# Two-layer hybrid trunk: gate, branch and first-layer products written feature-major, and another order of columns at the head of the second layer

## The chip, the cores and the metric

The kernel runs on one core of one Trainium2 chip. The metric is device microseconds of one execution, the median of several runs. Everything is 32-bit floating point on the way in and out; matrix products are made in a rounded 32-bit type (fp32r in the profile), with each operand split into a high and a low part.

## The reference

Two layers work on 256 positions of width 1024. Each layer first mixes, then applies an MLP:

```
mod = silu(c) @ ada_w[l] + ada_b[l]            # sh1, sc1, g1, sh2, sc2, g2
h = rms_norm(x) * (1 + sc1) + sh1
proj = h @ w_in   # u, v | fox q k v f | moba q k v | ssm z, xbc, dt | gates
y_a = gelu(u) * (causal spatial product of layer_norm(gelu(v)))
y_b = forgetting attention(fox q, k, v, f)
y_c = causal attention with partial rotary (moba q, k, v)
y_d = Mamba-2 mixer(z, xbc, dt)
merged = sum_i sigmoid(gate_i) * (y_i @ w_branch_i)
x = x + g1 * (merged @ w_out)
x = x + g2 * (relu(rms_norm'(x) @ w1)^2 @ w2)
```

The output is the final RMSNorm of x.

## The kernel before, in words

**Weights.** All large weights come in units of 0.5 MB: two blocks of 128 rows by 512 columns. `stream()` lists them in the order of use, and between them the units of `ada_w`, which VectorE folds into an accumulator (`acc`, line 242). Each weight unit lands in one of five `raw` buffers, ScalarE casts it to its high part (`hi`, line 363) and VectorE subtracts to get its low part (`lo`, line 365). `ahead` fetches three units ahead of the one in use, six in four places where tiles of later stages are lent to it (`lent`: `hl`, `hq`). A chunk is four units: 1024 rows by 512 columns.

**Two forms of product.** With activations split as `xh`, `xl` and weights as `hi`, `lo`, each product is xh·hi + xh·lo + xl·hi. In the straight form (`gemm`, `unit_mms`, lines 419 to 421) the 128 by 128 activation block is the stationary operand and 512 weight columns stream past: 12 matmuls of 512 columns in a unit, and the result has positions on the partitions. In the turned form (`gemm_T`, lines 447 to 449) a 128 by 128 block of the weight is stationary and the 256 positions stream past: 24 matmuls of 256 columns in a unit, and the result has features on the partitions, all positions in the free axis. The chunks `z1` to `z3` of both layers, `z0` of the second, `fq`, `fk` and six of eight `w1` chunks are turned already. `by_tile` runs several straight chunks for the first 128 positions, then again for the second 128, so that the second half of the activations may come later.

**Order of a layer.** u, v (first layer: together with z0, in steps; second layer: `by_tile`), z0 to z3 (input of Mamba), `narrow`, then q, k, v of forgetting attention (`fq`, `fk`, `fv`), then four times `branch`: two gate chunks (`ga0`, `ga1`), and the branch's own products (`pa0`, `pa1`), in the order a (gMLP), d (Mamba), b, c (`mq`, `mk`, `mv` lie between d and b), then `o0`, `o1` (w_out) and the MLP. `add` (lines 1103 to 1106) multiplies a branch's product with its gate and adds it to the sum `mg`, which has positions on the partitions. In branch c, `merge_T` transposes `mg` on TensorE in eight groups of four (tile `mT`), and lines 1145 and 1146 split the result into `xhT` and `xlT`, the activations of `o0` and `o1`.

**Generators.** Mixers are Python generators: `start` enters one in the list `running`, and `pump`, called behind each unit of a product, steps all of them. `yield n` waits n units more. So Mamba's parts stand in the program as many units behind one another as units are pumped, and `drain(gen_d)`, called behind the gates of branch d, writes whatever of Mamba is left in one go. Mamba ends with a broadcast product `rb` (line 914), six multiplications from it (line 917) and the split into `yhd` and `yld` (lines 521 and 522), which branch d's products `pd0` and `pd1` read.

Each engine works in the order of its program. PSUM tiles of the products come from a pool of four banks (`gps`), those of the mixers from a pool of two (`xps`), transposes from another two.

Of the kernel before, what the change touches and what calls it, by code (L numbers as in the profile page):

```python
# [15 lines left out]
P = 128  # L16
# [27 lines left out]
def stream():  # L44
# [16 lines left out]
    for l in range(L):  # L61
# [23 lines left out]
        for nm, c0 in (("fq", C_FQ), ("fk", C_FK), ("fv", C_FV)):  # L85
            plan_chunk((l, nm), "w_in", l, c0, KT)
# [52 lines left out]
def trunk_kernel(ctx: ExitStack, tc: tile.TileContext, a: dict, out: bass.AP):  # L139
# [295 lines left out]
    def gemm_T(key, xs, alloc):  # L435

        ps = [alloc(f"pT_{key[0]}{key[1]}_{q}").rearrange("p (f c) -> p f c", f=2) for q in range(2)]
        for u in range(KT // 2):
            i = take(key, 1)[0]
            ahead(i)  # L440
            hi, lo = ready[i]
            for f in range(4):
                o = ps[f // 2][:, f % 2, :]
                for j in range(2):
                    k = 2 * u + j
                    c = slice(f * P, (f + 1) * P)
                    te.matmul(o, hi[j][:, c], xs[0][:, k, :], start=k == 0 and f % 2 == 0, stop=False)  # L447
                    te.matmul(o, hi[j][:, c], xs[1][:, k, :], start=False, stop=False)  # L448
                    te.matmul(o, lo[j][:, c], xs[0][:, k, :], start=False, stop=k == KT - 1 and f % 2 == 1)  # L449
            pump()  # L450
        return ps
# [65 lines left out]
    def yT_tiles(nm, n, tag):  # L517
        return by_pos([mp.tile([P, n, NT * P], F32R, tag=tag, bufs=2, name=f"y{w}{nm}") for w in "hl"])
# [123 lines left out]
    def qkv(l, nm, hT, rot):  # L642
# [11 lines left out]
        ps = gemm((l, nm + "v"), KT, hT)  # L654
        vt = []
        for t in range(NT):
            vt.append(tok(f"{nm}v{l}{t}"))
            s.copy(vt[t], ps[t])
# [3 lines left out]
    def gmlp(l, ps, ya):  # L662
        pr = params[l]
        us, vn = [], []
        for which, lst in ((0, us), (1, vn)):
            for t in range(NT):
                tk = tok(f"{'uv'[which]}{l}{t}")
                s.activation(tk, ps[which][t], AF.Gelu_apprx_tanh)
                lst.append(tk)
# [10 lines left out]
        for t in range(NT):  # L680
# [10 lines left out]
            uT = transposes(us[t], f"uT{l}{t}")  # L691
            v.tensor_tensor(tm, tm, uT, op=ALU.mult)
# [3 lines left out]

    def zx_post(l, n, ps, zs, xb):
        tks = []
        for t in range(NT):
            tk = tok(f"zx{l}{n}{t}")  # L700
            s.copy(tk, ps[t])
            tks.append(tk)
        yield 1
        for t in range(NT):
            tp = transposes(tks[t], f"zxT{l}{n}{t}")
            for lo_, hi_ in ((0, 2), (2, 4)):
                f0 = 4 * n + lo_
                if f0 < 6:
                    s.copy(zs[:, f0:f0 + 2, t * P:(t + 1) * P], tp[:, lo_:hi_, :])
                else:  # L710
                    s.copy(xb[:, f0 - 6:f0 - 4, 3 + t * P:3 + (t + 1) * P], tp[:, lo_:hi_, :])
            yield 0
# [301 lines left out]
    for l in range(L):  # L1014
        pr = params[l]
        res = {}
        if l == 0:
            full = fullp
            firsts = {nm: [gps(f"ps_0{nm}_{t}") for t in range(NT)] for nm in "uv"}

            def first_mms(f, nm, ts=range(NT)):
                if ts[0] == 0:
                    got[nm] = take((0, nm), 1)[0]
                for t in ts:
                    unit_mms(got[nm], t, firsts[nm][t], hT[t][0], hT[t][1], 2 * f - 2, f == 1, f == 4)

            got = {}
            for f in range(5):
# [22 lines left out]
                if f == 0:  # L1051
                    fetch_one()
                    firsts["z0"] = [xps(f"ps_0z0_{t}") for t in range(NT)]
# [18 lines left out]
        ya = yT_tiles(f"a{l}", 4, "y2")  # L1072
# [3 lines left out]
        yd = yT_tiles(f"d{l}", 6, "y3")  # L1076
        zx = []
        if pz is not None:
            zx = [start(zx_post(l, 0, pz, zs, xb), -1)]
# [8 lines left out]
        qT, kT, vt = qkv(l, "f", hT, False)  # L1088
        mg = [mp.tile([P, D], F32, tag="mg", bufs=2, name=f"mg{l}{t}") for t in range(NT)]

        def gates(br, n):
            pgt = gemm((l, f"g{br}{n}"), KT, hT)
            th = []
            for t in range(NT):
                h = tok(f"th{l}{br}{n}{t}")
                s.activation(h, pgt[t], AF.Tanh, scale=0.5)
# [3 lines left out]
        def add(br, n, t, th, pp):  # L1100
            dst = mg[t][:, n * 512:n * 512 + 512]
            if br == "a":
                v.scalar_tensor_tensor(dst, th[t], 1.0, pp[t], op0=ALU.add, op1=ALU.mult)
            else:
                v.scalar_tensor_tensor(th[t], th[t], 1.0, pp[t], op0=ALU.add, op1=ALU.mult)
                v.tensor_tensor(dst, dst, th[t], op=ALU.add)

        def branch(br, ys, before=None, last=None):
            ths = [gates(br, n) for n in range(2)]
            if before is not None:  # L1110
                before()
            if last is not None:
                def after(n):
                    def f(t, ps):
                        add(br, n, t, ths[n], {t: ps})
                        last(t, n)
                    return f
# [189 lines left out]
```

## Time and profile before

| | |
|---|---|
| runs | 1119.17, 1122.38, 1124.32 us; median 1122.38 |
| profiled execution | 1119.5 us, its span 1117.5 us |
| TensorE (PE) | 1089.8 us busy, 98% of the span, 6420 matmuls |
| weight loads of TensorE (PEld) | 913.2 us, 82% |
| VectorE (DVE) | 767.5 us, 69% |
| ScalarE (ACT) | 619.7 us, 55% |
| DMA | 234.62 MB, mean 210 GB/s |
| granted TensorE clock | 0.996 of full speed |

TensorE's busy time counts overlapping matmuls once; whether it advances at its full pace is read from the distance between the starts of its instructions, not from the share.

### The profile page before, as it was taken

What the parts mean: (1) busy time and instruction counts of PE and PEld (TensorE: products, weight loads), DVE (VectorE), ACT (ScalarE), POOL (GpSimd) and SP (SyncE); (2) the same over time, 40 slices, a digit from 0 to 9 for tenths busy, and PEclk for the clock granted to TensorE, in tenths of its full rate; (3) what the DMA queues carried; (4) which work ended last, traced back from release to release, by engine and by line L of the source; (5) the groups of instructions that cost most, each with busy time, mean ns of one, the idle gap of its engine ahead of it and who ended that gap; (6) DMA issues with size and microseconds to landing.
All of it is one profiled execution on the core that took longest, in us unless ns stands there. A gap on an engine that the chain in (4) does not pass through costs nothing.

```text
span 1117.5 us, 16674 instructions
## 1 busy us (share of the span) xinstructions
PE 1089.8 (98%) x6420; PEld 913.2 (82%) x6420; DVE 767.5 (69%) x1088; ACT 619.7 (55%) x975; POOL 37.2 (3%) x58
## 2 busy tenths in 40 slices
PE   6999999999999999999899999999999999999997
PEld 4799977777777789988788998777777777889985
DVE  3887657786778756566676685678768676555565
ACT  4566565565555555554464575656555456554463
POOL 0000002000000100000000000110000001000000
PEclk9999999999999999999999999999999999999999
DMA  9876553666666668677845655446666755666670
GB/s 373 310 234 188 186 173 133 199 226 200 226 218 224 197 206 287 230 262 256 294 155 185 211 175 169 167 148 213 221 209 208 236 187 180 190 206 227 206 245 38
DMA packets 65327, 234.62 MB, mean 210 GB/s; under 512 B 7256, under 2 KB 8024, under 8 KB 65248
## 3 DMA queue, kind: packets, MB, share of 16 engines
q1 hardware_dynamic: 64960, 233.30, 63.7%
q8 instruction: 50, 0.82, 0.3%
q10 hardware_dynamic: 288, 0.27, 0.1%
q14 instruction: 29, 0.24, 0.1%
HBM read 232.49 MB, written 1.05 MB: 209 GB/s over the span
## 4 chain that ended last, share of the span: by engine, by line
PE 81%; DMA 8%; DVE 7%; ACT 2%; issue 2%; POOL 1%; DVEq 0%; POOLq 0%; ACTq 0%; SPq 0%
DMA raw<-in_wpk_dram 7%; PE yps L419 4%; PE yps L420 4%; PE yps L421 4%; DVE lo L365 2%; PE pT_1w L447 2%; PE pT_1w L448 2%; PE pT_1w L449 2%; PE pT_1z L447 1%; PE pT_1z L448 1%; PE pT_1z L449 1%; PE pT_0w L449 1%; PE pT_0w L447 1%; PE pT_0w L448 1%; PE pT_0z L447 1%
## 5 line engine op out<-in xcount | busy, mean ns | idle before, releaser
L363 ACT CAST hi<-raw 128x1024 fp32r<-128x1024 f32 x319 | 333.7, 1050 | 323.7 <-PE yps L421 60.2
L365 DVE TENSOR_TENSOR lo<-raw,hi 128x1024 fp32r<-128x1024 f32 x315 | 382.2, 1222 | 159.4 <-ACT hi L363 158.4
L242 DVE SCALAR_TENSOR_TENSOR acc<-raw,csil,acc 128x1024 f32<-128x1024 f32 x70 | 89.9, 1284 | 93.2 <-DMA raw<-in_wpk_dram 93.1
L420 PE MATMUL yps<-lo,hh 128*128 128x512 f32 x232 | 91.7, 395 | 0.5 <-DVE lo L365 0.5
L419 PE MATMUL yps<-hi,hh 128*128 128x512 f32 x232 | 92.0, 397 | 0.0
L421 PE MATMUL yps<-hi,hl 128*128 128x512 f32 x232 | 91.6, 395 | 0.0
L449 PE MATMUL pT_0w<-xhT,lo 128*128 128x256 f32 x192 | 54.2, 282 | 0.1
L447 PE MATMUL pT_1w<-xhT,hi 128*128 128x256 f32 x192 | 54.0, 281 | 0.0
L447 PE MATMUL pT_0w<-xhT,hi 128*128 128x256 f32 x192 | 54.0, 281 | 0.0
L449 PE MATMUL pT_1w<-xhT,lo 128*128 128x256 f32 x192 | 53.9, 281 | 0.0
L448 PE MATMUL pT_1w<-xlT,hi 128*128 128x256 f32 x192 | 53.9, 281 | 0.0
L448 PE MATMUL pT_0w<-xlT,hi 128*128 128x256 f32 x192 | 53.9, 281 | 0.0
L419 PEld LDWEIGHTS yps<-hi,hh 128*128 128x128 f32 x232 | 43.5, 188 | 10.9 <-issue 1.0
L420 PEld LDWEIGHTS yps<-lo,hh 128*128 128x128 f32 x232 | 43.5, 187 | 10.7 <-DVE lo L365 0.9
L421 PEld LDWEIGHTS yps<-hi,hl 128*128 128x128 f32 x232 | 43.5, 187 | 10.6
L449 PEld LDWEIGHTS pT_0w<-xhT,lo 128*128 128x128 f32 x192 | 36.2, 188 | 0.5 <-DVE lo L365 0.5
L448 PEld LDWEIGHTS pT_1w<-xlT,hi 128*128 128x128 f32 x192 | 36.2, 188 | 0.3
L448 PEld LDWEIGHTS pT_0w<-xlT,hi 128*128 128x128 f32 x192 | 36.2, 188 | 0.3
L447 PEld LDWEIGHTS pT_0w<-xhT,hi 128*128 128x128 f32 x192 | 36.2, 188 | 0.3
L447 PEld LDWEIGHTS pT_1w<-xhT,hi 128*128 128x128 f32 x192 | 36.2, 188 | 0.3
L447 PE MATMUL pT_1z<-xhT,hi 128*128 128x256 f32 x128 | 36.3, 284 | 0.0
L449 PEld LDWEIGHTS pT_1w<-xhT,lo 128*128 128x128 f32 x192 | 36.2, 188 | 0.0
(608 smaller groups left out, 2760.5 us busy)
## 6 DMA issues: line engine op xcount, KB each, us to landing
raw<-in_wpk_dram SPq DMA_DIRECT2D x436, 512.0 KB, 4.3
x<-in_x_dram SPq DMA_DIRECT2D x2, 512.0 KB
wst<-in_big_dram SPq DMA_DIRECT2D x2, 512.0 KB
out_dram<-xnz SPq DMA_DIRECT2D x4, 256.0 KB
bsb<-in_big_dram SPq DMA_DIRECT2D x2, 256.0 KB
fw<-in_final_norm_w_dram SPq DMA_DIRECT2D x1, 512.0 KB
w<-in_big_dram SPq DMA_DIRECT2D x2, 128.0 KB
cst<-in_cst_dram ACTq DMA_DIRECT2D x1, 185.0 KB
```

What stands on the lines that cost most here:

```text
L242: v.scalar_tensor_tensor(acc[l, j], raw, csil[:, k:k + 1], acc[l, j], op0=ALU.mult, op1=ALU.add)
L363: s.copy(hi, raw)
L365: v.tensor_sub(lo, raw, hi.bitcast(F32))
L419: te.matmul(ps, xhi[:, k, :], hi[j], start=first and j == 0, stop=False)
L420: te.matmul(ps, xhi[:, k, :], lo[j], start=False, stop=False)
L421: te.matmul(ps, xlo[:, k, :], hi[j], start=False, stop=last and j == 1)
L447: te.matmul(o, hi[j][:, c], xs[0][:, k, :], start=k == 0 and f % 2 == 0, stop=False)
L448: te.matmul(o, hi[j][:, c], xs[1][:, k, :], start=False, stop=False)
L449: te.matmul(o, lo[j][:, c], xs[0][:, k, :], start=False, stop=k == KT - 1 and f % 2 == 1)
```

## The change

Five things are done.

1. The eight gate chunks and the eight branch products of each layer are made in the turned form (`gemm_T` with a count of row blocks `nk`). So are u and z0 of the first layer and u of the second. The branch products read a mixer's whole tile (`yaw`, `ydw`, ...) where they read it by halves of the positions.
2. `mg` now has features on the partitions, one tile for each half of the features. `merge_part` scales and splits it straight into `xhT` and `xlT`; the eight groups of transposes `mT` are gone, and so is `by_tile` for branch c.
3. u comes out with features on the partitions, as the spatial product does: the four groups of transposes `uT` are gone; the product with u is two instructions of half the size.
4. z0 of the first layer is treated as the other z chunks are (`turned_post`): the two groups of transposes `zxT` and the copies ahead of them are gone.
5. In the second layer `by_tile` runs v and `fv`, where it ran u and v; u follows, turned, in the banks of `xps`; `fv` no longer stands behind `fk`.

```diff
@@ stream()
-            for nm, c0 in (("u", C_U), ("v", C_V), ("z0", C_Z)):
+            for nm, c0 in (("v", C_V), ("fv", C_FV), ("u", C_U), ("z0", C_Z)):
                 plan_chunk((l, nm), "w_in", l, c0, KT)
@@
-        for nm, c0 in (("fq", C_FQ), ("fk", C_FK), ("fv", C_FV)):
+        for nm, c0 in (("fq", C_FQ), ("fk", C_FK), ("fv", C_FV))[:3 if l == 0 else 2]:
@@
+    def turned_banks(key, alloc):
+        return [alloc(f"pT_{key[0]}{key[1]}_{q}").rearrange("p (f c) -> p f c", f=2) for q in range(2)]
+
+    def unit_T(i, ps, xs, kt0, nk, fs=range(4)):
+        hi, lo = ready[i]
+        for f in fs:
+            o = ps[f // 2][:, f % 2, :]
+            for j in range(2):
+                k = kt0 + j
+                c = slice(f * P, (f + 1) * P)
+                te.matmul(o, hi[j][:, c], xs[0][:, k, :], start=k == 0 and f % 2 == 0, stop=False)
+                te.matmul(o, hi[j][:, c], xs[1][:, k, :], start=False, stop=False)
+                te.matmul(o, lo[j][:, c], xs[0][:, k, :], start=False, stop=k == nk - 1 and f % 2 == 1)
+
+    def gemm_T(key, xs, alloc=gps, nk=KT):
+
+        ps = turned_banks(key, alloc)
+        for u in range(nk // 2):
             i = take(key, 1)[0]
             ahead(i)
...
+            unit_T(i, ps, xs, 2 * u, nk)
             pump()
@@ gmlp
-            uT = transposes(us[t], f"uT{l}{t}")
-            v.tensor_tensor(tm, tm, uT, op=ALU.mult)
+            for q in range(2):
+                v.tensor_tensor(tm[:, 2 * q:2 * q + 2, :], tm[:, 2 * q:2 * q + 2, :], us[q][:, :, t * P:(t + 1) * P],
+                                op=ALU.mult)
@@ trunk, first layer
                 for t in ts:
+                    if nm != "v":
+                        unit_T(got[nm], firsts[nm], xall, 2 * f - 2, KT, (2 * t, 2 * t + 1))
+                        continue
                     unit_mms(got[nm], t, firsts[nm][t], hT[t][0], hT[t][1], 2 * f - 2, f == 1, f == 4)
@@ trunk, second layer
-            pu, pv, pz = [], [], None
+            pv, pf, pz = [], [], None
             by_tile([((l, nm), 4, hT, lambda t, nm=nm: gps(f"ps_{l}{nm}_{t}"), True, True,
-                      lambda t, ps, lst=lst: lst.append(ps)) for nm, lst in (("u", pu), ("v", pv))])
+                      lambda t, ps, lst=lst: lst.append(ps)) for nm, lst in (("v", pv), ("fv", pf))])
+            vt = []
+            for t in range(NT):
+                vt.append(tok(f"fv{l}{t}"))
+                s.copy(vt[t], pf[t])
+            pu = gemm_T((l, "u"), xall, xps)
@@
-            zx = [start(zx_post(l, 0, pz, zs, xb), -1)]
+            zx = [start(turned_post(pz, [zs[:, f:f + 2, :] for f in (0, 2)]), -1)]
@@ gates, add, branch
-            pgt = gemm((l, f"g{br}{n}"), KT, hT)
+            pgt = gemm_T((l, f"g{br}{n}"), xall)
...
-        def add(br, n, t, th, pp):
-            dst = mg[t][:, n * 512:n * 512 + 512]
+        def add(br, n, q, th, pp):
+            dst = mg[n][:, 2 * q:2 * q + 2, :]
...
             for n in range(2):
-                pp = gemm((l, f"p{br}{n}"), branches[br][1], ys)
-                for t in range(NT):
-                    add(br, n, t, ths[n], pp)
+                pp = gemm_T((l, f"p{br}{n}"), ys, nk=branches[br][1])
+                for q in range(2):
+                    add(br, n, q, ths[n], pp)
+                    if last is not None:
+                        last(n, q)
@@ merged sum
-        def merge_T(t, q):
-            tp = transposes(mg[t][:, q * 512:q * 512 + 512], f"mT{l}{t}{q}")
-            s.activation(mT[t][0][:, 4 * q:4 * q + 4, :], tp, AF.Copy, scale=0.5)
...
+        def merge_part(n, q):
+            f = slice(4 * n + 2 * q, 4 * n + 2 * q + 2)
+            part = mg[n][:, 2 * q:2 * q + 2, :]
+            s.activation(xall[0][:, f, :], part, AF.Copy, scale=0.5)
+            v.scalar_tensor_tensor(xall[1][:, f, :], part, 0.5, xall[0][:, f, :].bitcast(F32), op0=ALU.mult,
+                                   op1=ALU.subtract)
```

**What moves: the end of Mamba in the second layer, on TensorE.** `rb1` is Mamba's last product, `gd` and `pd` are gates and products of branch d, `scf` the scores of forgetting attention. Before, `rb1` stood behind the last unit of `gd0`, ahead of the whole chunk `gd1`:

```order
L421 MATMUL ps_1gd0_1_7185<-hi291_7188,xlT_96 128x512
L914 MATMUL rb1_7265<-dg1_7227,onesr_85 128x512
L419 MATMUL ps_1gd1_0_7277<-hi292_7206,xhT_95 128x512
L420 MATMUL ps_1gd1_0_7277<-lo292_7207,xhT_95 128x512
L421 MATMUL ps_1gd1_0_7277<-hi292_7206,xlT_96 128x512
```

Now:

```order
L447 MATMUL pT_1gd1_1_8147<-xhT_95,lo295_8151 128x256
L907 MATMUL rb1_8275<-dg1_8213,onesr_85 128x512
L549 MATMUL scf1000_8393<-rff1000_8323,va1_7626 128x512
L555 MATMUL scf1000_8393<-fkT1_7357,fqT1_7191 128x128 x4
L558 LDWEIGHTS identb_83
L558 MATMUL scf1000_8393<-mask_646,identb_83 128x512
L549 MATMUL scf1001_8394<-rff1001_8328,va1_7626 128x512
L555 MATMUL scf1001_8394<-fkT1_7357,fqT1_7191 128x128 x4
L558 LDWEIGHTS identb_83
L558 MATMUL scf1001_8394<-mask_646,identb_83 128x512
L445 MATMUL pT_1pd0_0_8291<-yhd1_6484,hi296_8180 128x256
L445 MATMUL pT_1pd0_1_8292<-yhd1_6484,hi296_8180 128x256
```

`rb1` has moved from behind `gd0` to behind `gd1`, since four fewer units are pumped between Mamba's start and branch d; the first scores, which stood behind the three units of `pd0`, now stand ahead of them. The tile `scf1001` has the PSUM bank that `rb1` had.

**What moves: the merged sum of the first layer.** On VectorE before (`th` times product, `mg` sum, `xlT` low part of the merged activations, `lo` and `hq` of the weights of `o0` and `o1`, `acc` an `ada_w` unit):

```order
L1146 SCALAR_TENSOR_TENSOR xlT_96<-mT000_3407,xhT_95 128x4x128
L1106 TENSOR_TENSOR mg00_1511<-mg00_1511,th0c10_3369 128x512
L242 SCALAR_TENSOR_TENSOR acc04_2610<-raw141_3501,csil_110,acc04_2610 128x1024
L1105 SCALAR_TENSOR_TENSOR th0c01_3262<-th0c01_3262,ps_0pc0_1_3422 128x512
L1146 SCALAR_TENSOR_TENSOR xlT_96<-mT001_3429,xhT_95 128x4x128
L1106 TENSOR_TENSOR mg01_1512<-mg01_1512,th0c01_3262 128x512
L365 TENSOR_TENSOR lo136_3451<-raw136_3448,hi136_3450 128x1024
L365 TENSOR_TENSOR lo137_3457<-raw137_3454,hi137_3456 128x1024
L1146 SCALAR_TENSOR_TENSOR xlT_96<-mT010_3480,xhT_95 128x4x128
L1105 SCALAR_TENSOR_TENSOR th0c11_3371<-th0c11_3371,ps_0pc1_1_3447 128x512
L365 TENSOR_TENSOR lo142_3507<-raw142_3504,hi142_3506 128x1024
L1106 TENSOR_TENSOR mg01_1512<-mg01_1512,th0c11_3371 128x512
```

Now:

```order
L1141 SCALAR_TENSOR_TENSOR xlT_96<-mg00_1583,xhT_95 128x512
L1107 TENSOR_TENSOR mg00_1583<-mg00_1583,th0c01_3838 128x512
L1106 SCALAR_TENSOR_TENSOR th0c10_3993<-th0c10_3993,pT_0pc1_0_4070 128x512
L242 SCALAR_TENSOR_TENSOR acc04_2994<-raw141_4160,csil_110,acc04_2994 128x1024
L1141 SCALAR_TENSOR_TENSOR xlT_96<-mg00_1583,xhT_95 128x512
L1107 TENSOR_TENSOR mg01_1584<-mg01_1584,th0c10_3993 128x512
L1106 SCALAR_TENSOR_TENSOR th0c11_3995<-th0c11_3995,pT_0pc1_1_4071 128x512
L365 TENSOR_TENSOR lo142_4166<-raw142_4163,hi142_4165 128x1024
L1141 SCALAR_TENSOR_TENSOR xlT_96<-mg01_1584,xhT_95 128x512
L1107 TENSOR_TENSOR mg01_1584<-mg01_1584,th0c11_3995 128x512
```

The kinds of work are the same; each half of the features now goes through `th`, `mg` and `xlT` behind the other. On TensorE, the transposes that stood between `pc1` and `o0`:

```order
L420 MATMUL ps_0pc1_1_3447<-lo134_3389,yhc0_2766 128x512
L421 MATMUL ps_0pc1_1_3447<-hi134_3388,ylc0_2767 128x512
L527 MATMUL mT010_3480<-cst_81,mg01_1512 128x128 x4
L419 MATMUL ps_0o0_0_3489<-hi136_3450,xhT_95 128x512
L419 MATMUL ps_0o1_0_3563<-hi142_3506,xhT_95 128x512
L420 MATMUL ps_0o0_0_3489<-lo136_3451,xhT_95 128x512
```

Now:

```order
L446 MATMUL pT_0pc1_1_4071<-ylc0_3151,hi134_4031 128x256
L447 MATMUL pT_0pc1_1_4071<-yhc0_3150,lo134_4032 128x256
L419 MATMUL ps_0o0_0_4148<-hi136_4074,xhT_95 128x512
L420 MATMUL ps_0o0_0_4148<-lo136_4075,xhT_95 128x512
L421 MATMUL ps_0o0_0_4148<-hi136_4074,xlT_96 128x512
L419 MATMUL ps_0o0_0_4148<-hi136_4074,xhT_95 128x512
```

`o0` follows `pc1` directly, and its first rows read what is made of the first half of the features.

## Rows read from the trace of the kernel before

**Rows 1.** The page, busy time by engine, and the granted clock in 40 slices.

```profile
PE 1089.8 (98%) x6420; PEld 913.2 (82%) x6420; DVE 767.5 (69%) x1088; ACT 619.7 (55%) x975; POOL 37.2 (3%) x58
...
PEclk9999999999999999999999999999999999999999
```

**Rows 2.** Waits of PE, whole run: waiter, releaser: us in total, times, longest.

```profile
PE mT L527 <- DVE mg L1106: 2.2, 3, 1.0
```

**Rows 3.** Timeline of PE, second layer, fq to fv: start us, us, instruction.

```profile
648.30 0.28 PE L447 MATMUL pT_1fq<-xhT,hi 128*128 128x256 f32 x1
...
671.02 0.40 PE L419 MATMUL ps_1fv<-hi,xhT 128*128 128x512 f32 x1
...
682.22 0.29 PE L779 MATMUL nar<-cat,cst 128*128 128x20 f32 x2
```

**Rows 4.** Timeline of PE around one group of transposes, first layer.

```profile
71.97 0.28 PE L449 MATMUL pT_0z<-xhT,lo 128*128 128x256 f32 x1
72.09 0.60 PE L527 MATMUL zxT<-cst,zx 128*128 128x128 f32 x4
...
72.65 0.28 PE L448 MATMUL pT_0z<-xlT,hi 128*128 128x256 f32 x1
```

**Rows 5.** Tiles of the removed transposes: count, duration ns, first and last start.

```profile
L527 PE MATMUL mT<-cst,mg x32: 270/272/302, 346.9 to 904.9; 128*128 128x128 f32 x32
...
L527 PE MATMUL zxT<-cst,zx x8: 271/272/273, 68.4 to 72.4; 128*128 128x128 f32 x8
...
L527 PE MATMUL uT<-cst,u x16: 272/273/328, 79.3 to 622.6; 128*128 128x128 f32 x16
```

**Rows 6.** Timeline of all engines behind rb, second layer.

```profile
742.17 1.02 PE L914 MATMUL rb<-dg,onesr 128*128 128x512 f32 x2
...
743.23 2.44 DVE L917 SCALAR_TENSOR_TENSOR xb<-xb,par,rb 128x256 f32<-128x256 f32 x6 [1.31 <-PE rb L914]
...
745.58 1.22 DVE L365 TENSOR_TENSOR lo<-raw,hi 128x1024 fp32r<-128x1024 f32 x1
...
746.98 1.58 ACT L521 CAST yhd<-xb 128x768 fp32r<-128x768 f32 x2
...
748.25 1.82 DVE L522 TENSOR_TENSOR yld<-xb,yhd 128x768 fp32r<-128x768 f32 x2
```

**Rows 7.** Timeline of PE around the first scores, second layer.

```profile
762.63 0.63 PE L542 MATMUL scf<-rff,va 80*128 80x512 f32 x2
...
764.96 0.39 PE L420 MATMUL ps_1pd<-lo,yhd 128*128 128x512 f32 x1
```

**Rows 8.** Timeline of ACT, DVE and PE at the first unit of u.

```profile
17.67 0.71 ACT L521 CAST xhT<-full 128x256 fp32r<-128x256 f32 x2
...
18.51 0.76 DVE L522 TENSOR_TENSOR xlT<-full,xhT 128x256 fp32r<-128x256 f32 x2
...
18.13 0.50 PE L419 MATMUL ps_0u<-hi,xhT 128*128 128x512 f32 x1 [1.01 <-ACT xhT L521]
...
18.99 0.73 PE L421 MATMUL ps_0u<-hi,xlT 128*128 128x512 f32 x1
```

**Rows 9.** Merged sum, first layer: windows (busy us by engine), a piece of DVE's timeline, and waits of DVE.

```profile
343.00:362.50 19.50, 17.89 (x88) 13.29 (x87) 17.87 (x23) 11.15 (x14) 0.00 (x0) 1.00 0.68 222
...
350.80 1.28 DVE L242 SCALAR_TENSOR_TENSOR acc<-raw,csil,acc 128x1024 f32<-128x1024 f32 x1
351.99 0.68 DVE L1105 SCALAR_TENSOR_TENSOR th0c<-th0c,ps_0pc 128x512 f32<-128x512 f32 x1
352.59 0.68 DVE L1146 SCALAR_TENSOR_TENSOR xlT<-mT,xhT 128x512 fp32r<-128x512 f32 x1
...
DVE acc L242 <- DMA raw<-in_wpk_dram: 93.1, 56, 4.5
```

**Rows 10.** Timeline of PE at its longest wait, end of the first layer.

```profile
555.09 1.11 PE L274 MATMUL sst<-cst,ssr 128*128 128x128 f32 x4 [3.27 <-ACT ssr L270]
...
557.28 0.63 PE L419 MATMUL yps<-hq,hh 128*128 128x512 f32 x1
```

More of the change, by code (lines that the diff above doesn't have):

```diff
@@ L517, in yT_tiles @@
     def yT_tiles(nm, n, tag):
[L518 removed]
+        y = [mp.tile([P, n, NT * P], F32R, tag=tag, bufs=2, name=f"y{w}{nm}") for w in "hl"]
+        return y, by_pos(y)
     def hilo(hi, lo, src):
@@ L665, in gmlp @@
         for which, lst in ((0, us), (1, vn)):
-            for t in range(NT):
+            for t in range(2):
                 tk = tok(f"{'uv'[which]}{l}{t}")
-                s.activation(tk, ps[which][t], AF.Gelu_apprx_tanh)
-                lst.append(tk)
+                s.activation(tk, ps[which][t].rearrange("p f c -> p (f c)") if which == 0 else ps[which][t],
+                             AF.Gelu_apprx_tanh)
+                lst.append(tk.rearrange("p (f c) -> p f c", f=2) if which == 0 else tk)
         yield 0
@@ L1018, in trunk_kernel @@
             full = fullp
-            firsts = {nm: [gps(f"ps_0{nm}_{t}") for t in range(NT)] for nm in "uv"}
+            firsts = {"u": turned_banks((0, "u"), gps), "v": [gps(f"ps_0v_{t}") for t in range(NT)]}
             def first_mms(f, nm, ts=range(NT)):
@@ L1052, in trunk_kernel @@
                     fetch_one()
-                    firsts["z0"] = [xps(f"ps_0z0_{t}") for t in range(NT)]
+                    firsts["z0"] = turned_banks((0, "z0"), xps)
                 if f > 0:
@@ L1108, in branch @@
-        def branch(br, ys, before=None, last=None):
+                v.scalar_tensor_tensor(th[q], th[q], 1.0, pp[q], op0=ALU.add, op1=ALU.mult)
+                v.tensor_tensor(dst, dst, th[q], op=ALU.add)
+        def branch(br, ys, prior=None, last=None):
             ths = [gates(br, n) for n in range(2)]
[L1110 to L1117, printed above, removed]
-                by_tile([((l, f"p{br}{n}"), branches[br][1] // 2, ys, lambda t, n=n: gps(f"ps_{l}p{br}{n}_{t}"), True,
-                          True, after(n)) for n in range(2)])
-                return
-            for n in range(2):
-                pp = gemm((l, f"p{br}{n}"), branches[br][1], ys)
-                for t in range(NT):
-                    add(br, n, t, ths[n], pp)
@@ L1126, in trunk_kernel @@
-        branch("a", ya)
+            if prior is not None:
+                prior()
+            for n in range(2):
+                pp = gemm_T((l, f"p{br}{n}"), ys, nk=branches[br][1])
+                for q in range(2):
+                    add(br, n, q, ths[n], pp)
+                    if last is not None:
+                        last(n, q)
+        branch("a", yaw)
         if l + 1 < L:
             load_par(l + 1, nc.sync)
-        yb = yT_tiles(f"b{l}", 4, "y2")
+        ybw, yb = yT_tiles(f"b{l}", 4, "y2")
```

74 lines of the change are left out of this document (19 added, 55 removed).

## The prediction

> **What bounds the kernel now.** I read the page first, then the waits of TensorE, then its timeline in the stretches that the change touches. The page shows TensorE busy for 98% of the span at the full granted clock, VectorE for 69%, ScalarE for 55% [rows 1]. Busy matmuls need not be matmuls at their pace, so the timeline decides: in the first layer's and the second's products, starts follow each other at one fixed distance, and the waits of TensorE that the change could remove come to 2.2 us in all [rows 2]. So the end of the run is set by TensorE's list of instructions nearly everywhere. A microsecond taken off that list is a microsecond gained, and a new wait on it is lost in full. That VectorE, ScalarE or DMA get less to do counts only where TensorE waits for them.
>
> **The change part by part.**
>
> *The turned form costs a little.* In the second layer fq and fk, two turned chunks, run from 648.30 to 671.02, 11.36 us each; fv, a straight one of the same size, from 671.02 to 682.22, 11.20 us [rows 3]. Nothing else stands in those stretches. So a chunk of four units costs 0.16 us more when turned. The change turns 28 chunks: eight gate chunks a layer (16), 18 units of branch products a layer (36 units, 9 chunks), u and z0 of the first layer (2), u of the second (1). 28 x 0.16 = **4.5 us more**, all of it on TensorE. The Trainium skill, page "TensorE: Matmul & The Clock Gate", section "Back-to-back issue gap", gives a matmul N columns at 2.4 GHz and 2.5 ns on top; by that rule 48 more matmuls in a chunk cost 0.12 us, and the term would be 3.4 us (an estimate from that page). The rows say 0.16, and I take them.
>
> *Transposes go.* One group of four transposes between products takes from 72.09 (where the next matmul would have begun) to 72.65 less one turned matmul (118 ns, 11.36 us by 96): 0.44 us [rows 3, 4]. The groups removed: 32 transposes mT, 16 uT and 8 zxT make 8, 4 and 2 groups [rows 5]. 14 x 0.44 = 6.2 us, and TensorE's waits ahead of mT, 2.2 us [rows 2], go with them: **8.4 us less**. The copies behind zxT and the larger product with u lie on ScalarE and VectorE beside TensorE's work and count nothing. If the 2.2 us come back as another wait, that is the term on the merged sum below.
>
> *The merged sum.* `o0` now follows `pc1` directly. Let T be the end of `pc1`. The first half of the features is complete on TensorE 5.7 us before T, its first quarter 7.1 us before T (a chunk's 11.36 us by 96 a matmul). VectorE then has, in its order, 12 steps of `th`, `mg` and `xlT` at 0.60 us from start to start, one `acc` at 1.19, three `lo` at 1.22 and two `hq`, half a `lo` each [rows 6, 9]: 13.3 us, so it ends near T + 6.3. TensorE wants the last `xlT` behind 20 matmuls of `o0` and five of `o1` (233 ns each, 11.20 us by 48 [rows 3]), that is at T + 5.8 and later by the small products for `ada_w` that stand between. The second quarter is wanted behind eight matmuls, at T + 1.9; VectorE's first ten steps have it ready near T + 0.8. So the cover holds by about 1 us if VectorE starts on time. But VectorE was busy for 17.87 of 19.50 us there [rows 9], so I take 0.25 us a layer, **0.5 us more** (between 0 and the 2.2 us of the nearest rows, the waits ahead of mT).
>
> *fv leaves, and Mamba ends late in the second layer.* Four units fewer are pumped between Mamba's start and branch d, so `rb` lands directly ahead of `pd0`. Before, the chain behind `rb` lay under gd1: `rb` from 742.17, six steps on VectorE from 743.23 for 2.44 us, `yhd` 1.58 us on ScalarE, `lo` 1.22 and `yld` 1.82 us on VectorE [rows 6]. Now TensorE stands behind it. With X the start of `rb`: the six steps end at X + 3.5, `yhd` at X + 5.1, `lo` at X + 4.7, `yld` (it needs both) near X + 6.6, and only then does pd0 go on. In these 6.6 us TensorE has: `rb`, 1.0; the scores, from 762.63 to 764.96 less one straight matmul, 2.1 [rows 7]; four matmuls of pd0 that read `yhd` alone, 0.47. The second half of the scores also waits for the six steps, since it has rb's bank, but that lies inside the 6.6. Idle: 6.6 - 3.6 = **3.0 us more**. Bounds: 1.8 if ScalarE's copy of the first half lets `yld` begin early, 5.4 if one `lo` more stands in front and the clock falls as behind the longest wait of the run: there TensorE waited 3.27 us, and straight matmuls then last 0.63 us instead of 0.40 [rows 3, 10]. The idle time here is split into pieces by the scores, so I take no fall.
>
> *u after v and fv.* z0 of the second layer gets the banks of fv's two tiles, which ScalarE copies early; v and fv give the second half of the norm the same 11.2 us of cover as u and v did. The gelus of u stand ahead of v's now, but only z1 needs v's banks, one chunk later. **Nothing.** If z0 had to wait for them, TensorE would stand for a few ScalarE steps there.
>
> *The first unit of u.* A turned matmul reads both halves of the positions. The first now waits for both `xhT` (18.38 instead of 18.1), the next for both `xlT` (19.27), where the first use of `xl` was at 18.99 [rows 8]: **0.4 us more** (0.25 to 0.8). In the three later rounds z0, 2.8 us, stands between and covers it.
>
> **The sum:** 4.5 - 8.4 + 0.5 + 3.0 + 0.4 = 0.0 us. On the profiled execution that leaves its 1119.5 us; it is 2.9 us under the median of the runs, and on that median I forecast **1122.4 us**: no change. Under 0.5%, 5.6 us, a measurement of this kernel can't tell a difference from none.
>
> **The rivals.**
>
> *The new waits don't come.* If VectorE and ScalarE run through the late end of Mamba under the scores, and the first unit and the merged sum cost nothing, what is left is 4.5 - 8.4 = -3.9 us, 1118.5. For: every wait of TensorE outside the ends of layers is short now. Against: the chain behind `rb` is measured and has no cover written behind it. Chance 0.19. To be faster by over 5.6 us, one of the old long waits must vanish with them, above all the 3.27 us at the end of the first layer [rows 10]: -7.2 us, 1115.2. The order of the work around it is unchanged, so 0.07.
>
> *VectorE sets the pace at the merged sum: slower.* The place is `acc` between `th` and `xlT`, in both layers. An `ada_w` unit that lands late holds all of VectorE's chain, and `o0` behind it. Such waits are 1.7 us in the mean (93.1 by 56), 4.5 at the longest [rows 9]. The point from which it decides is the slack of about 1 us above: a wait of 4.5 us in both layers costs 2 x 3.5 = 7 us, and the run ends at 1129.4; at the mean it costs 1.4 us and stays within no change. For: VectorE is the fullest there, and TensorE no longer has transposes to pass the time. Against: in the first layer before, this step began without a wait [rows 9]. Chance 0.14.
>
> *Turned products are slower than the rows of fq and fk.* The Trainium skill, the same page, section "The mechanism" with the list of what overlaps, has weight loads overlap running matmuls only where the row groups differ. As a mechanism of this kernel: the turned form loads weights twice as often, 28 x 48 = 1344 loads more, and if none lay under a matmul, at 142 ns each (913.2 us by 6420 [rows 1]) they would cost 191 us, 1313 us in all. Against it: in fq and fk a matmul starts every 118 ns, less than such a load takes, with a load for each [rows 3]. By that rule they could not. Chance 0.01.
>
> **How the numbers follow.** Forecast 0.59, no new waits 0.19, an old wait gone 0.07, VectorE's pace 0.14, weight loads 0.01. Faster by over 0.5%: 0.07 for the old wait, and 0.03 of the second case where its runs lie low, 0.10. Slower by over 0.5%: two thirds of VectorE's case (0.09), 0.01 for the loads, and 0.06 of the forecast where Mamba's end reaches its upper bound and the merged sum its own (2.4 + 1.7, and some wait more): 0.16. Within: 0.74. The range goes from 1117 (the waits gone, 1118.5, less half the spread of the runs) to 1130 (VectorE's case).
>
> **What would show it.** Each turned chunk 11.36 us; no mT, uT, zxT; TensorE idle some 3 us between the second layer's `rb` and `pd0`; no wait at z0 of the second layer; first `xlT` of the merged sum ahead of TensorE's need. Wrong I'd be if TensorE waits over 2 us at `o0` in a layer, if turned gates run slower than fq, or if the wait at pd0 is missing.

## The result and the profile after

The changed kernel takes 1134.14 us (median of four runs, 1130.39 to 1135.39), the kernel before 1121.68 beside it: ratio 1.0114, 95% interval 1.009 to 1.0138, so 12.5 us slower. The forecast was 1122.4 and its range ended at 1130. A second measurement gave 1.0113. The profiled execution took 1135.39 us, its span 1133.5, which is 16.0 us over the span of before; it is the slowest of the four, so its rows show a little more than the median does.

From the page of the changed kernel, busy time and granted clock:

```profile
PE 1098.3 (97%) x7708; PEld 983.7 (87%) x7708; DVE 766.7 (68%) x1092; ACT 617.9 (55%) x971; POOL 36.4 (3%) x58
...
PEclk9999999999999999999899999999999989999998
```

Against [rows 1] nothing on this page looks alarming: 8.5 us more of TensorE, the others as before, and three slices in which the clock dips. Where the time went shows in TensorE's timeline, cut at the first matmul of each step (us; the 11.20 us of the second layer's `fv`, which moved from behind `fk` to the head of the layer, are left out of both kernels):

| stretch | before | after | more |
|---|---|---|---|
| start to first u | 18.13 | 19.93 | +1.80 |
| u to `fq` | 83.18 | 82.19 | -0.99 |
| `fq` to `mq` | 124.82 | 125.90 | +1.08 |
| `mq` to `pc0` | 114.35 | 116.26 | +1.91 |
| `pc0` to `o0` | 14.41 | 11.36 | -3.05 |
| `o0` to `w10` | 25.26 | 28.32 | +3.06 |
| `w10` to second layer's `fq` | 268.17 | 269.70 | +1.53 |
| `fq` to `mq` | 113.63 | 119.27 | +5.64 |
| `mq` to `pc0` | 113.17 | 113.96 | +0.79 |
| `pc0` to `o0` | 13.53 | 15.48 | +1.95 |
| `o0` to `w10` | 25.27 | 27.63 | +2.36 |
| `w10` to the end | 192.42 | 192.36 | -0.06 |

Each column is one execution. Two of the rows scatter by themselves: over the kernel before and its variants below with a straight first u, the first stretch took 18.13 to 19.91 us, and that from `w10` to `fq` 265.5 to 269.7.

Two places stand out: the merged sum (`pc0` to `w10`), which was to gain about 5 us over both layers and lost 4.3, and the second layer's end of Mamba. TensorE's waits name both. Columns: what waited, for whom, us in total, times, longest.

```profile
PE ps_1o L419 <- ACT xhT L1140: 4.0, 1, 4.0
PE sst L274 <- ACT ssr L270: 2.7, 1, 2.7
...
PE mqt L534 <- DVE mqT L638: 1.7, 1, 1.7
PE ps_0o L419 <- ACT xhT L1140: 1.5, 1, 1.5
...
PE nar L719 <- DVE narr L715: 1.1, 1, 1.1
PE scf L549 <- DVE xb L910: 1.0, 1, 1.0
```

The waits ahead of `mT` [rows 2] are gone; larger ones stand one step later, at `o0`, for `xhT`.

**The merged sum of the second layer.** VectorE's timeline there (start, duration, line, operation; in brackets the idle time before it and what ended it):

```profile
901.81 1.28 DVE L242 SCALAR_TENSOR_TENSOR acc<-raw,csil,acc 128x1024 f32<-128x1024 f32 x1 [3.62 <-DMA raw<-in_wpk_dram]
903.01 1.22 DVE L365 TENSOR_TENSOR lo<-raw,hi 128x1024 fp32r<-128x1024 f32 x1
904.15 1.22 DVE L365 TENSOR_TENSOR hl<-raw,hl 128x1024 fp32r<-128x1024 f32 x1
905.28 1.22 DVE L365 TENSOR_TENSOR lo<-raw,hi 128x1024 fp32r<-128x1024 f32 x1
906.42 0.68 DVE L1106 SCALAR_TENSOR_TENSOR th1c<-th1c,pT_1pc 128x512 f32<-128x512 f32 x1
...
908.98 0.68 DVE L1107 TENSOR_TENSOR mg<-mg,th1c 128x512 f32<-128x512 f32 x1
...
913.54 0.69 DVE L1141 SCALAR_TENSOR_TENSOR xlT<-mg,xhT 128x512 fp32r<-128x512 f32 x1 [2.15 <-ACT xhT L1140]
```

`acc`, which folds a unit of `ada_w`, stands 3.62 us idle until its weights have landed. Everything behind it slides: the first `th` begins at 906.42. `pc1` ends at 909.45 (its last start and the 0.12 us from start to start), so that is 3.0 us ahead of its end, where the prediction had 7.1. In the first layer `acc` waited 1.52 us and `th` began 5.3 us ahead. Then ScalarE, which makes `xhT`:

```profile
907.71 1.05 ACT L363 CAST hi<-raw 128x1024 fp32r<-128x1024 f32 x1
911.93 1.04 ACT L363 CAST hi<-raw 128x1024 fp32r<-128x1024 f32 x1 [3.18 <-DMA raw<-in_wpk_dram]
912.89 0.62 ACT L1140 ACTIVATE xhT<-mg 128x512 fp32r<-128x512 f32 x1
```

The sum's first quarter is ready at 909.66 (908.98 and 0.68). But the cast of one more weight unit stands ahead of `xhT` in ScalarE's queue, waits 3.18 us for its own transfer, and `xhT` comes at 912.89. TensorE:

```profile
909.33 0.27 PE L447 MATMUL pT_1pc<-yhc,lo 128*128 128x256 f32 x1
913.56 0.79 PE L419 MATMUL ps_1o<-hi,xhT 128*128 128x512 f32 x1 [3.96 <-ACT xhT L1140]
914.16 0.63 PE L420 MATMUL ps_1o<-lo,xhT 128*128 128x512 f32 x1
914.58 0.63 PE L421 MATMUL ps_1o<-hi,xlT 128*128 128x512 f32 x1
...
920.93 0.39 PE L419 MATMUL ps_1o<-hi,xhT 128*128 128x512 f32 x1
```

Behind the wait the matmuls of `o0` last 0.63 us instead of 0.39, and follow each other at some 0.43 instead of 0.23, until 920. Mean granted clock by stretch (us, then busy time and count of each engine, PEclk, DMA share, GB/s):

```profile
900.00:909.00 9.00, 9.00 (x79) 9.00 (x78) 6.45 (x7) 4.00 (x4) 0.00 (x0) 1.00 0.68 241
909.00:914.00 5.00, 1.04 (x7) 0.85 (x6) 2.85 (x5) 2.07 (x4) 0.00 (x0) 0.87 0.91 327
914.00:921.00 7.00, 7.00 (x23) 3.76 (x23) 7.00 (x11) 4.18 (x8) 0.00 (x0) 0.61 0.36 110
```

DMA is 91% busy while TensorE waits, and 94% from 898 to 902, while VectorE waits for `acc`'s unit. But the queue had not been full all along. In two stretches near it almost nothing moved (DMA share 0.03 and 0.11):

```profile
893.00:895.00 2.00, 2.00 (x27) 1.85 (x25) 1.84 (x2) 0.88 (x1) 0.00 (x0) 1.00 0.03 10
902.00:904.00 2.00, 2.00 (x19) 2.00 (x18) 2.00 (x2) 0.96 (x2) 0.00 (x0) 1.00 0.11 39
```

In each of them VectorE has just begun an `acc` that had to wait for its unit (893.16 and 901.81). By the profile the next transfer is issued only when this `acc` is done. The waits for `acc` of SP, which issues the transfers, from 893 to 904:

```profile
SPq L314 <- DVE acc L242: 2.6, 2, 1.3
```

So an `acc` that waits for a late unit also makes the next units late.

**Mamba's end in the second layer.** TensorE:

```profile
759.57 1.02 PE L907 MATMUL rb<-dg,onesr 128*128 128x512 f32 x2
...
763.21 0.47 PE L549 MATMUL scf<-rff,va 80*128 80x512 f32 x1 [0.98 <-DVE xb L910]
...
764.74 0.82 PE L445 MATMUL pT_1pd<-yhd,hi 128*128 128x256 f32 x4
765.99 0.58 PE L446 MATMUL pT_1pd<-yld,hi 128*128 128x256 f32 x1 [0.43 <-DVE yld L529]
766.38 0.42 PE L447 MATMUL pT_1pd<-yhd,lo 128*128 128x256 f32 x1
766.59 0.41 PE L445 MATMUL pT_1pd<-yhd,hi 128*128 128x256 f32 x1
```

The chain runs as predicted: `pd0` goes on 6.4 us behind the start of `rb`. The idle pieces that the profile names are 0.98 and 0.43 us; the short products between them fill the rest. Then 15 matmuls run at half clock:

```profile
766.00:769.30 3.30, 3.30 (x15) 3.30 (x16) 3.27 (x8) 2.20 (x12) 0.00 (x0) 0.50 0.27 108
```

### The profile page after: what moved, and what is told of

Same layout as the page of the kernel before. It is cut to its first block, busy times and chain, and to the rows that moved or that the text cites. A ratio compares the mean times of both kernels' runs of the same rounds, so it can differ in the third digit from the quotient of the medians.

```text
span 1133.5 us, 19252 instructions
## 1 busy us (share of the span) xinstructions
PE 1098.3 (97%) x7708; PEld 983.7 (87%) x7708; DVE 766.7 (68%) x1092; ACT 617.9 (55%) x971; POOL 36.4 (3%) x58
## 3 DMA queue, kind: packets, MB, share of 16 engines
HBM read 232.49 MB, written 1.05 MB: 206 GB/s over the span
## 4 chain that ended last, share of the span: by engine, by line
PE 85%; DMA 6%; DVE 4%; ACT 3%; issue 2%; POOL 1%; DVEq 0%; POOLq 0%; ACTq 0%; SPq 0%
DMA raw<-in_wpk_dram 5%; PE yps L419 5%; PE yps L421 5%; PE yps L420 5%; PE pT_1w L445 2%; PE pT_1w L447 2%; PE pT_1w L446 2%; DVE lo L365 2%; PE pT_0w L445 1%; PE pT_0w L446 1%; PE pT_0w L447 1%; PE pT_0z L445 1%; PE pT_0z L446 1%; PE pT_0z L447 1%; PE pT_1z L445 1%
## 5 line engine op out<-in xcount | busy, mean ns | idle before, releaser
L445 PE MATMUL pT_0z<-xhT,hi 128*128 128x256 f32 x128 | 36.4, 284 | 0.0
```

## The experiments

First theory: the loss is Mamba's late end (3.0 us and 1.4 to 1.6 of slow clock) and, at `o0`, weights that land late, held against TensorE by the cast ahead of `xhT`. Ratios are to the kernel before; 0.001 is 1.1 us.

**Mamba four pumps earlier in the second layer.**

```diff
-        start(gen_d, 4)
+        start(gen_d, 4 if l == 0 else 0)
```

> The changed kernel with Mamba of the second layer started four pumps earlier, so that rb no longer stands directly ahead of pd0. Theory (the late end of Mamba costs 3.0 us of waiting and the fall of the clock behind it another 1.4 to 1.6): the wait and the slow matmuls behind rb go, 4.6 us less than the changed kernel, near 1129.5 us. Rival (what was lost there comes back elsewhere, since VectorE's work only moves): within 1 us of the changed kernel, 1134.

1.0041 (1.0023 to 1.006), 8.1 us below the changed kernel's 1.0113. The stretch `fq` to `mq` falls from 119.27 to 114.68 us, 4.59 less, as expected, and no wait is left at `pd0`. The rest of the 8.1 lies in the scatter of the two medians and at the sum: there TensorE waited 0.6 us in the first layer's `o0` and 2.1 in the second's, with the order of work unchanged.

**No units of `ada_w` among `pc` and `o0`.** The numbers are weights: `stream()` spreads a fixed count of `ada_w` units over the chunks in proportion to them, so a 0.0 moves units to the other chunks.

```diff
-                     ("gc", 0.45), ("pc", 0.45), ("o0", 0.45), ("f", 0.0)):
+                     ("gc", 0.45), ("pc", 0.0), ("o0", 0.0), ("f", 0.0)):
```

> The changed kernel with no unit of ada_w placed among pc and o0. They are read and used elsewhere; o1's weights come from memory sooner. Theory (ScalarE's cast of a late weight unit of o1 stands in its queue ahead of the xhT of the merged sum, and TensorE waits for that at o0): TensorE's waits at the start of o0, 1.5 us in the first layer and 4.1 in the second, fall below 0.5 us each and the slow matmuls behind them go: 5 to 9 us less, 1125 to 1129 us. Rival (VectorE's chain of th, mg and xlT is too long by itself): the waits stay at 1 to 4 us, and the time within 2 us of 1134.

1.0047 (1.0031 to 1.0064), 7.4 us less. The waits at the start of `o0` are gone. VectorE, then TensorE, of this kernel:

```profile
902.56 0.68 DVE L1106 SCALAR_TENSOR_TENSOR th1c<-th1c,pT_1pc 128x512 f32<-128x512 f32 x1
```

```profile
909.07 0.28 PE L447 MATMUL pT_1pc<-yhc,lo 128*128 128x256 f32 x1
909.19 0.40 PE L419 MATMUL ps_1o<-hi,xhT 128*128 128x512 f32 x1
...
912.91 0.50 PE L421 MATMUL ps_1o<-hl,xlT 128*128 128x512 f32 x1 [0.30 <-DVE xlT L1141]
```

With nothing to wait for, `th` begins 6.6 us ahead of the end of `pc1`, near the 7.1 of the prediction, and VectorE's chain just holds, with 0.3 us missing once. But the units went elsewhere: a wait of 2.9 us for `mkT` is new in the first layer. The edit takes away `acc` on VectorE and lets the weight units behind it come sooner, so it doesn't tell VectorE's queue from ScalarE's.

**Part 5 alone**, in the kernel before; u stays straight.

```diff
-            for nm, c0 in (("u", C_U), ("v", C_V), ("z0", C_Z)):
+            for nm, c0 in (("v", C_V), ("fv", C_FV), ("u", C_U), ("z0", C_Z)):
...
-                      lambda t, ps, lst=lst: lst.append(ps)) for nm, lst in (("u", pu), ("v", pv))])
+                      lambda t, ps, lst=lst: lst.append(ps)) for nm, lst in (("v", pv), ("fv", pf))])
+            pu = gemm((l, "u"), KT, hT, alloc=xps)
```

> The kernel before with the second layer's change of order alone: v and fv lead tile by tile, u straight behind them, no fv behind fk; no gate, product or merged sum is turned and z0 of the first layer is as before. Theory: rb of the second layer lands late as in the changed kernel, with its wait and slow clock: 4 to 5 us more than the kernel before, 1126 to 1127 us. Rival (the late end only costs together with the turned form of pd0): within 1 us of the kernel before, 1121 to 1122.

1.0031 (1.0012 to 1.0049), 3.5 us more. `fq` to `mq` takes 116.52 us, 2.89 more than before's 113.63: the 3.0 of the prediction, without a fall of the clock (1.00 from 745 to 760 us, around the end of Mamba). So the lead alone costs what was predicted. The slow clock came with the turned form: it fell to half at this place in all five profiled executions that have the late end and the turned `pd0`, and not in this one, the only one that has the late end and the straight form.

**Both edits**, Mamba earlier and no units at `pc` and `o0`.

> Mamba four pumps earlier in the second layer and no unit of ada_w among pc and o0, together. Theory (the two places are the whole of the loss, and independent): 4.6 us and 5 to 9 us less than the changed kernel, 1120 to 1125 us, within 0.4% of the kernel before. Rival (one place hides the other, or VectorE's chain stays): 1129 to 1134 us.

1.0003 (0.9986 to 1.002): the whole loss is gone, and nothing is gained over the kernel before. A wait for `mkT`, 3.1 us, stands in the first layer.

**Who makes `xhT`: VectorE, or GpSimd.** The split is the line with `AF.Copy` in `merge_part`.

```diff
-            s.activation(xall[0][:, f, :], part, AF.Copy, scale=0.5)
+            v.tensor_scalar(xall[0][:, f, :], part, 0.5, None, op0=ALU.mult)
```

> The changed kernel with the rounded high half of the merged sum (xhT) made by VectorE instead of ScalarE; nothing else differs. Theory (the xhT stood on ScalarE behind the cast of a weight unit that came late): the waits at the first matmul of o0, 1.5 and 4.1 us, fall under 1 us; VectorE has 2.4 us more per layer, so that up to 1 us comes back inside o0; 2 to 6 us less than the changed kernel, 1128 to 1132 us. Rival (VectorE's chain is the limit): the waits grow by 1 to 2.4 us each, 1136 to 1139 us.

1.009 (1.0069 to 1.0111), 2.6 us less: in the theory's span by its time, but not by its rows. TensorE still waited 0.6 and 1.7 us, now for VectorE, whose `acc` had waited 3.81 us for its unit. So ScalarE's queue is not the cause by itself; the late units hold either queue. The gain itself is not clear of noise: the intervals of 1.009 and 1.0113 overlap.

With `g.tensor_scalar` in the same line:

> The same with xhT of the merged sum made by GpSimd, which has an empty queue there. Theory (ScalarE's queue): the wait at the first o0 becomes what one such step takes on GpSimd, 1.2 us for 256 elements in the trace, so 2.4 us or so for 512, ahead of each xlT; 0 to 4 us less than the changed kernel, 1130 to 1134 us. Rival (VectorE's chain): the waits stay and get 1 to 2 us longer, 1136 to 1140 us.

1.0156 (1.0131 to 1.018): 4.8 us more. The waits at `o0` came to 1.1 and 2.9 us, and VectorE's order changed too; an `acc` now held TensorE 2.2 us. That is about the rival's time, but by other waits than it names.

**Where else the units of `ada_w` could go**, with Mamba earlier and, in the first two, 0.0 for `pc` and `o0`: among the chunks z (0.4 raised to 0.7 and 0.625), among `gb`, `pb`, `gc` (each 0.18 more), or out of `pc` and `o0` in the second layer alone.

```diff
-            return 0.0 if key == (0, "z0") else 0.4
+            return 0.0 if key == (0, "z0") else (0.4 + 3.6 / 12 if l == 0 else 0.4 + 3.6 / 16)
```

> Mamba four pumps earlier, no unit of ada_w among pc and o0, and the units that this displaces placed among the chunks z instead of among the heads' products mq, mk, mv. Theory (of the 12.4 us that the two undone places gave back, 3 went into the new wait for mkT in the first layer): that wait of 3.1 us goes, 2 to 4 us less than the version without the last step, 1116 to 1118.5 us, 0.2 to 0.4% below the kernel before. Rival (VectorE or the norm among the chunks z has no room): a new wait there of 1 to 3 us, 1119 to 1122 us.

1.0032 (1.0017 to 1.0048). In the profiled execution, the slowest of ten, the wait for `mkT` fell to 1.4 us, and one of 1.7 us for `narr` came at the second layer's start. (The wait for `ssr` at the end of the first layer is 3.9 us there, but 3.3 in the kernel before.) By its time the rival holds.

```diff
-                return r
+                return r + 0.18 if c in ("gb", "pb", "gc") else r
```

> Mamba four pumps earlier, no unit of ada_w among pc and o0, and the displaced units spread evenly over the chunks gb, pb and gc ahead of them; the heads' products mq, mk and mv keep what they have in the changed kernel. Theory (3 us of what the two places give back went into the wait for mkT): the wait for mkT of 3.1 us goes and nothing new comes, since VectorE waits for weights in gb to gc: 2 to 4 us less than the version that left these units to the heads' products, 0.997 to 0.999 of the kernel before. Rival (weights come too late wherever two units are read for one chunk's time, so the waits move to gc and pc): 1.000 to 1.004.

1.0013 (0.9996 to 1.0029), the rival's side. The wait for `mkT` went; 1.1 us came back inside `o0` for `xlT`, in three waits.

```diff
-                     ("gc", 0.45), ("pc", 0.0), ("o0", 0.0), ("f", 0.0)):
+                     ("gc", 0.45), ("pc", 0.45 - 0.45 * l), ("o0", 0.45 - 0.45 * l), ("f", 0.0)):
```

> Mamba four pumps earlier, and units of ada_w taken from pc and o0 in the second layer only; the first layer stands as in the changed kernel. Theory (the first layer's wait at o0 of 0.6 to 1.5 us and some slow matmuls cost about what the wait for mkT costs): within 2 us of the version that takes them from both layers, 0.999 to 1.002 of the kernel before. Rival (the first layer's o0 is the smaller loss): 0.997 to 0.999.

1.0002 (0.9987 to 1.0017): as expected.

**The changed kernel once more.**

> The changed kernel once more, beside the others. Theory: 1.0 to 1.3% over the kernel before, as at first; the waits at o0 differ from execution to execution, since they hang on when a weight unit lands (in the version with Mamba earlier the first layer's was 0.6 us instead of 1.5, with the same order of work). Rival (the first runs were on a slow chip): within 0.5% of the kernel before.

1.0113 (1.009 to 1.0136). In this execution, of 1125.62 us, the waits at `o0` were 1.2 and 1.7 us instead of 1.5 and 4.0.

**The same edit on the kernel before.**

```diff
-                     ("gc", 0.45), ("pc", 0.45), ("o0", 0.45), ("f", 0.0)):
+                     ("gc", 0.45), ("pc", 0.0), ("o0", 0.0), ("f", 0.0)):
```

> The kernel before with no unit of ada_w placed among pc and o0, and nothing else: the same edit that took 7 us off the changed kernel. Theory (the straight pc and the transposes, with 2.2 us of waits in all, leave the late weight units time to land; only the turned sum is short of it): at most the 2.2 us of waits go and up to 3 us come with the wait for mkT: 0.998 to 1.003 of the kernel before. Rival (the units cost the same in any form, and the change is not what made them dear): 0.993 to 0.996.

0.9954 (0.9939 to 0.9969), 1116.44 us: 5 us faster, and the rival's side. So the late units cost the kernel before 5 us, where the same edit took 7.4 off the changed one; with the scatter of the medians the two can't be told apart. This run beats both kernels. It also says that the edit's gain on the changed kernel can't all be booked to the change, and that the version with both edits, level with the kernel before, still stands 0.5% above the kernel before with this one edit.

So what does the turned sum itself cost? Three more runs; the first makes gates, branch products and sum turned in the kernel before, and leaves u, z0 and the lead as they were.

```diff
-            pgt = gemm((l, f"g{br}{n}"), KT, hT)
+            pgt = gemm_T((l, f"g{br}{n}"), xall)
...
-                pp = gemm((l, f"p{br}{n}"), branches[br][1], ys)
+                pp = gemm_T((l, f"p{br}{n}"), ys, nk=branches[br][1])
...
-               last=lambda t, n: start(merge_gen(t, n), 0 if t == 0 else 1))
+        branch("c", ycw, prior=lambda: drain(gen_c[0]), last=merge_part)
```

> The kernel before with gates, branch products and merged sum turned, and nothing else: u, z0, the order in which the second layer leads and Mamba's place are as before. By the terms of the prediction: 25 turned chunks, 4.0 us more; eight groups of transposes, 3.5 us, and 2.2 us of waits less; the merged sum 0.5 us more: 0.999 of the kernel before. Theory now (the turned sum gives back its gain and more in waits on late weights): 1.002 to 1.006. Rival (what is left of the loss sits in u, z0 and the lead of v and fv): 0.997 to 1.000.

1.0053 (1.0035 to 1.0072): 5.9 us slower, where the prediction's terms made it 1.2 faster. Turned chunks add what they should (`fq` to `mq` 125.89 us, 1.07 more). The sum does not gain: TensorE waits 1.4 and 3.2 us at `o0`.

The second is the same with 0.0 for `pc` and `o0`, as above.

> The same with no unit of ada_w among pc and o0. Theory (the loss in the turned sum is waits on late weights there, which this takes away): below or at the straight kernel with the same edit, 0.993 to 0.996 of the kernel before. Rival (the turned chunks and VectorE's chain cost more than the transposes gave, late weights or not): 0.998 to 1.002, as the whole change with both edits stood 0.5% above the straight kernel with this one.

1.0044 (1.0022 to 1.0066), against 0.9954 for the straight form with that edit. By the time the theory is wrong, and the rival's span is passed as well. By the rows, the sum does gain now, and the loss is elsewhere; both layers' `pc0` to `w10` added up, us, one execution each:

| | with `ada_w` there | without |
|---|---|---|
| straight | 78.47 (before) | 74.53 |
| turned, sum alone | 80.01 | 72.36 |
| turned, the whole change | 82.79, again 77.92 | 71.16 |
| the same, Mamba earlier | 76.49 | 71.00 |

Without those units the turned sum is 2.2 to 3.5 us shorter than the straight one. What eats it is the first layer's `mq` to `pc0`: 121.77 us, 114.89 in the straight kernel with the edit, where turned chunks explain 0.8. TensorE of the turned kernel waits there, and behind the wait its granted clock is 0.50:

```profile
PE pTf L534 <- DVE mkT L638: 3.3, 1, 3.3
```

```profile
273.00:278.00 5.00, 4.60 (x15) 3.92 (x16) 2.61 (x3) 1.21 (x3) 0.00 (x0) 0.50 0.74 215
```

and VectorE shows why:

```profile
271.46 1.28 DVE L242 SCALAR_TENSOR_TENSOR acc<-raw,csil,acc 128x1024 f32<-128x1024 f32 x1 [2.85 <-DMA raw<-in_wpk_dram]
272.66 0.68 DVE L638 COPY mkT<-mkt 128x512 f32<-128x512 f32 x1
```

It is the same mechanism as at the sum: an `acc` with a late unit ahead of a copy that TensorE wants. In the straight kernel `acc` waits as long there (2.89 us), but VectorE is earlier against TensorE, the wait for `mkT` is 0.8, and the clock does not fall. The `acc` ahead of this one had waited 1.05 us in the turned kernel, 0.17 in the straight one. What made those units later was not settled, so the share of the turned form in this loss stays open.

**The lead of v and `fv` with Mamba earlier**: part 5 alone, and

```diff
-        start(gen_d, 4)
+        start(gen_d, 4 if l == 0 else 0)
```

> The kernel before with the lead of v and fv alone and Mamba of the second layer four pumps earlier. Theory (only the late end of Mamba made the lead cost 3 to 4 us): 0.998 to 1.001 of the kernel before. Rival (the lead itself costs, by the order in which the norm, the gelus and z0 now stand): 1.002 to 1.005.

1.0005 (0.9988 to 1.0022). `fq` to `mq` is 113.63, the figure of before to the hundredth.

## Why the prediction was wrong

*Turned chunks, +4.5: right.* `fq` to `mq` of the first layer has 6.5 chunks newly turned (four of gates, one of `pa`, one and a half of `pd`), 1.04 us by 0.16; the stretch grew by 1.08. The lower figure, 0.12 a chunk, an estimate from the Trainium skill, page "TensorE: Matmul & The Clock Gate", section "Back-to-back issue gap", would give 0.78; the page states that rule for the gap of an isolated matmul, and the trace sides with the rows. The rival of weight loads that don't overlap is ruled out by the same stretch.

*Transposes, -8.4: right in size, but not kept.* `pc0` to `o0` of the first layer fell by 3.05 us and the stretch with z0 by 0.99. Behind that the waits moved on by one step, as the prediction's last clause on this term had it ("come back as another wait").

*The merged sum, +0.5: the step that failed.* Its reckoning of VectorE's steps was near: without late units `th` starts 6.6 us ahead instead of 7.1, and 0 to 0.4 us a layer is missing (1.1 in the run with more units in `gb` to `gc`). Two things failed. The first is "if VectorE starts on time". I set this against the rival because "in the first layer before, this step began without a wait" [rows 9]. That row, the `acc` at 350.80, is the one inside the step, between `th` and `xlT`, and there nothing waited in the changed kernel either (356.86 and 915.35 in the first profile). The `acc` that sets when the first `th` begins stands ahead of it, and had waited in both layers of the kernel before:

```profile
341.95 1.28 DVE L242 SCALAR_TENSOR_TENSOR acc<-raw,csil,acc 128x1024 f32<-128x1024 f32 x1 [2.67 <-DMA raw<-in_wpk_dram]
886.51 1.28 DVE L242 SCALAR_TENSOR_TENSOR acc<-raw,csil,acc 128x1024 f32<-128x1024 f32 x1 [1.40 <-DMA raw<-in_wpk_dram]
```

There the first `th` still began 10.2 us ahead of the end of `pc`, since `by_tile` completes the first product after a quarter of the matmuls, with transposes and waits among the rest; the turned form has 7.1 us at the most. With its own waits at `acc` (1.52 and 3.62 us in the first profile, 1.65 and 3.31 in the second) `th` began 5.3 us ahead in the first layer of both, and 3.0 and 4.8 us in the second layer.

The second is ScalarE, whose part in the sum was put at nothing. In the second layer of the first profile VectorE had the sum's first quarter ready at 909.66, 0.2 us behind the end of `pc1`; most of the wait of 3.96 us is the cast that kept `xhT` until 912.89. With `xhT` on VectorE, though, 1.7 us of wait stayed, so the two shares change from execution to execution. The rival had the direction and the kind of cause, a late `ada_w` unit; it named the `acc` inside the step and lacked this second queue.

Over both layers the step cost 4.3 us more than before in the first profile, 0.55 less in the second, where it was to gain 4.9 (eight groups and their waits, 5.7, less 0.5 and 0.3 for turned `pc`). The prediction's own sign, a wait of over 2 us at `o0` in a layer, came in the first profile (3.96) and not in the second (1.18 and 1.66).

*Mamba's late end, +3.0: wait right, clock wrong.* The late end costs 2.89 us alone. With the turned `pd0` behind it the clock fell as well, 4.59 us in all by the rows. By the pairs of runs the late end is worth 8.1, 4.9 (with the other edit) and 2.9 us (the lead alone): about 5. "I take no fall" failed; a wait cut up by short products did not keep the clock up.

*u after v and `fv`, nothing: right.* No wait at z0, and the lead alone with Mamba earlier costs nothing. A wait of 1.1 us for `narr` at the second layer's start is new in the first profile, 0.4 in the second; its cause stays open. *The first unit of u, +0.4: within its bounds* (0.25 to 0.8), about 0.7. TensorE's wait ahead of it is 1.32 us instead of 1.01, and from its first matmul to the first of `wsum` it takes 0.67 more (45.93 us against 45.26), of which 0.32 belong to two turned chunks.

Added up by the first profile: 4.2 for the turned chunks outside the sum, about 5 for Mamba's end, 4.3 for the sum, 0.7 for the first unit, and 2.6 less for the six groups `uT` and `zxT`, 11.6 us. With the sum of the second profile it is 6.8. The medians say 12.5. Each pair of medians is uncertain by 2 to 3 us, and the sum alone differs by 4.9 between two executions, so the shares are not known better than that.

## What to carry to other kernels

Before counting a removed step as a gain on the bounding engine, ask what was getting ready meanwhile: here the next step's input stood behind late weights, and the time of the transposes turned into waiting for it. A wait for a transfer, seen in one place of one execution, is a sample, not a constant (here 1.66 and 3.96 us for the same instruction); take the mean over the whole profile as the term, and not as a rival. Low-priority work that waits for its own transfer (here `acc`) should not stand in a queue just ahead of a step that the bounding engine wants: taking it away there was worth 5 us in the kernel before. Where it goes instead has to be looked at in the same way: in the turned kernels it came back as a wait for `mkT`.

## What the hardware showed

The granted clock is not a function of the wait's length alone. Before, the wait of 3.27 us at the end of the first layer ended at 555.09 and was followed by a stretch at a mean clock of 0.66. With part 5 alone it was as long, 3.28 us, ended at 553.55, and the clock stayed at 1.00 behind it. The two kernels' rows of 5 us each:

```profile
555.00:560.00 5.00, 4.91 (x17) 4.13 (x18) 1.24 (x4) 0.04 (x1) 0.00 (x0) 0.66 0.63 216
```

```profile
555.00:560.00 5.00, 5.00 (x23) 4.08 (x22) 1.58 (x3) 0.72 (x2) 0.22 (x1) 1.00 0.40 151
```

And at `pd0` two waits of 0.98 and 0.43 us, with short products between, were followed by 3.3 us at half clock (1.2 of 2.4 GHz). By estimate, slow matmuls added 1.5 us there (15 of them in 3.3 us, at 0.12 us each at full clock) and about 2.4 behind the wait at `o0` (12 matmuls at 0.43 instead of 0.23). What decides is left open.
